# Triangular inversion in the second mixer: blocks of 16 on 128 partitions and three doublings, in place of blocks of 32 and two

## The chip, the cores and the metric

The kernel runs on one core of one Trainium2 chip, as one launch. The metric is the device time of the launch in microseconds (us): the median of the runs shown. A profile of one execution stands beside it.

## The reference

The model is two layers over 1024 tokens of width 1024; each layer is a mixer, a cross attention over a memory of 256 rows, and a squared-ReLU MLP. The second layer's mixer is a gated delta rule with 8 heads of 128 columns, worked in chunks of 64 tokens. What the change touches is the solve with a unit lower triangular matrix, one for each head and chunk:

```python
kk = jnp.einsum('nbhtd,nbhsd->nbhts', kc, kc)
lower = jnp.where(strict, bc[..., :, None] * kk * decay, 0.0)
rhs = jnp.concatenate([vc * bc[..., None], kc * (bc * jnp.exp(g))[..., None]], axis=-1)
sol = lax.linalg.triangular_solve(lower + eye, rhs, left_side=True, lower=True, unit_diagonal=True)
u_c, w_c = sol[..., :dv], sol[..., dv:]
...
v_new = u - jnp.einsum('bhtk,bhkv->bhtv', wk, S)
o = jnp.einsum('bhtk,bhkv->bhtv', qd, S) + jnp.einsum('bhts,bhsv->bhtv', att, v_new)
S = S * jnp.exp(gl)[..., None, None] + jnp.einsum('bhsk,bhsv->bhkv', kd, v_new)
```

## The kernel before

The kernel works in chunks of 128 tokens, so a head has 8 triangular matrices of 128 by 128. It forms the inverse of each, and the recurrence over the chunks then multiplies by it.

`mix_c` (L819) runs over the head pairs (0,1), (2,3), (4,5), (6,7). For a pair, `gdn_head` (L953) projects the heads' keys, queries and values on TensorE (PE; `proj`, `mm3`, L156 to L158), and `gdn_pre` (L984) convolves and scales them (VectorE, DVE, L1004 and L1008) and writes six operands of each chunk to DRAM (`Bd`), with the strictly upper triangular matrix U (the transpose of `lower`) in `Ud`. Then `gdn_inv` (L1092) inverts the pair, and for the first two pairs `gdn_rec` (L1145) runs the recurrence at once. The last two pairs run their recurrences together, as four heads, at the end; after them stand `c_gate` for the 8 heads (projections of the gate) and `mem_kv(1)` (keys and values of the memory), which need nothing of the inversion.

`gdn_inv` has two stages. In the first, the diagonal blocks of 32 by 32 of both heads are gathered from `Ud` to 64 partitions, one block on a partition (tile G, L1103). A second tile X begins as identity blocks (L1104, L1105). 31 steps of substitution follow, each of them two DVE instructions that depend on each other: a product into `pr` (L1109) and a subtraction from X (L1114). X is written to `Xd` in DRAM at the places of the diagonal blocks (L1116); the rest of `Xd` was zeroed once.

In the second stage each head is taken alone. X and U come back as 128 by 1024 tiles (L1122, L1123), the 32 by 32 blocks are transposed into Y (L1124), and two doublings follow, n = 32 and n = 64. A doubling is a chain of groups of 8 float32 matmuls with 64 moving columns, all of them through the one PSUM buffer of the tag `i`: U times X (L1129), a copy to a tile Z by ScalarE (ACT, L1132), for n = 32 alone Y times Z and a subtraction from X (L1136, L1137), then Z times Y and a subtraction from Y (L1140, L1141). So a head has five such groups. Y goes to `Bd` for the recurrence (L1088).

The order of instructions on each engine is fixed when the kernel is built: the tile framework schedules by its own timeline and mixes the inversion of one pair with the projections and convolutions of the next and with recurrences. On the chip each engine takes its instructions in that order, and one that waits holds up what is queued behind it. All DMAs here go out from the SP queue.

Of the kernel before, what the change touches and what calls it, by code (L numbers as in the profile page):

```python
# [11 lines left out]
F32 = mybir.dt.float32  # L12
# [14 lines left out]
class Model:  # L27
# [336 lines left out]
    def mix(self, l):  # L364
        if l == 0:
            with self.phase(
                dict(z=3, so=1, ml=2),
                **dict(kq=8, v=4, e=2, sp=2, sh=2, sl=1, wh=2, wl=1, A=2, ah=1, al=1, so_st=1),
            ):
                self.mix_start(l, "so", dict(M=3, W=2, V=2, N=4, C=1, st=1, gg=1, ot=1))  # L370
                self.mix_ab()
                self.out_parts(False)
                self.x_open(self.x_src)
                self.out_proj(self.a["ab_o"])
        else:
            with self.phase(
                dict(a=2, i=1, rec=2, o=1),
                **dict(X=3, Y=2, Uk=1, pr=1, B=4, y=3, S=4, on=2),
            ):
                self.first = [self.ldw(self.a["c_w"][i]) for i in (8, 0)]  # L380
                self.mix_start(l, "o", dict(raw=5, kq=2, vc=1, M=1, qe=1, ua=1, kv=2))
                self.mix_c()
                self.out_parts(True)
                self.x_open(self.x_src, (1,))
                self.out_proj(self.a["c_o"])
# [456 lines left out]
    def gdn_consts(self):  # L842
        nc, c = self.nc, self.ph

        self.cgain = c.tile([128, 1], F32, name="cgain")
        nc.sync.dma_start(out=self.cgain, in_=self.a["c_hg"])
        nc.vector.tensor_scalar_mul(self.cgain, self.cgain, 0.5)
        self.convw = c.tile([128, 96], F32, name="convw")
        nc.sync.dma_start(out=self.convw, in_=self.a["c_cw"])
        self.power = c.tile([128, 8], F32, name="power")  # L850
        nc.vector.memset(self.power[:, 0:4], 0.5)
        nc.vector.memset(self.power[:, 4:8], -0.5)

        self.zt = [c.tile([128, 1024], F32, name=f"zt{i}") for i in range(2)]
        for z in self.zt:
            nc.gpsimd.memset(z, 0.0)

        self.Ud = [self.dr.tile([8, 4 * 4128], F32, tag=f"Ud{h}", name=self.nm("Ud")) for h in range(8)]
        self.Xd = [self.dr.tile([8, 4 * 4128], F32, tag=f"Xd{h}", name=self.nm("Xd")) for h in range(4)]
        self.Bd = [self.dr.tile([8, 128, 6, 128], F32, tag=f"Bd{h}", name=self.nm("Bd")) for h in range(8)]  # L860
        for x in self.Xd:
            nc.sync.dma_start(out=self.dense(x), in_=self.zt[0].rearrange("p (c t) -> p c t", t=128))
# [2 lines left out]
        return d[:, :16384].rearrange("c (s t) -> s c t", t=128)  # L865

    def blocks(self, d):
        b = d.rearrange("c (b r) -> c b r", r=4128)[:, :, :4096]
        return b.rearrange("c b (i w) -> c b i w", w=128)[:, :, :, :32]

    def c_gate(self, h):

# [220 lines left out]
    def gdn_inv(self, heads):  # L1093

        nc = self.nc
        mm = nc.tensor.matmul
        n32 = 32 * len(heads)
        G = self.big("X")
        X = self.big("X")
        g3 = G[:n32].rearrange("p (s t) -> p s t", s=32)  # L1100
        x3 = X[:n32].rearrange("p (t c) -> p t c", t=32)
        for j, h in enumerate(heads):
            nc.sync.dma_start(out=g3[j * 32 : j * 32 + 32], in_=self.blocks(self.Ud[h]))  # L1103
        nc.gpsimd.memset(X[:n32], 0.0)  # L1104
        nc.gpsimd.memset(X[:n32, 0:1024:33], 1.0)  # L1105
        for s in range(31):
            n, w = 31 - s, s + 1
            pr = self.keep("pr", 256, F32)[:n32, : n * w].rearrange("p (t c) -> p t c", t=n)
            nc.vector.tensor_mul(  # L1109
                pr,  # L1110
                g3[:, s, s + 1 :].unsqueeze(2).broadcast_to([n32, n, w]),
                x3[:, s, :w].unsqueeze(1).broadcast_to([n32, n, w]),
            )
            nc.vector.tensor_sub(x3[:, s + 1 :, :w], x3[:, s + 1 :, :w], pr)  # L1114
        for j, h in enumerate(heads):
            nc.sync.dma_start(out=self.blocks(self.Xd[h % 4]), in_=x3[j * 32 : j * 32 + 32])  # L1116
        chunks = [slice(i * 128, i * 128 + 128) for i in range(8)]

        two = lambda t, n, i: t.rearrange("p (c b h t) -> p c b h t", c=8, b=64 // n, h=2)[:, :, :, i]
        for h in heads:  # L1120
            X, Y, U = self.big("X"), self.big("Y"), self.big("Uk")
            nc.sync.dma_start(out=X.rearrange("p (c t) -> p c t", t=128), in_=self.dense(self.Xd[h % 4]))  # L1122
            nc.sync.dma_start(out=U.rearrange("p (c t) -> p c t", t=128), in_=self.dense(self.Ud[h]))  # L1123
            nc.vector.transpose(Y, X)  # L1124
            for n, Z in zip((32, 64), self.zt):
                view = lambda t: t.rearrange("p (c b t) -> p c b t", c=8, b=64 // n)
                p = view(self.bank("i"))
                for c, s in enumerate(chunks):
                    mm(p[:, c], U[:, s], two(X, n, 0)[:, c], start=True, stop=True)  # L1129
                for b in range(64 // n):  # L1130
                    rows = slice((2 * b + 1) * n, (2 * b + 2) * n)
                    nc.scalar.copy(two(Z, n, 0)[rows, :, b], p[rows, :, b])  # L1132
                if n == 32:
                    p = view(self.bank("i"))
                    for c, s in enumerate(chunks):
                        mm(p[:, c], Y[:, s], two(Z, n, 0)[:, c], start=True, stop=True)  # L1136
                    nc.vector.tensor_sub(two(X, n, 0), two(X, n, 0), p)  # L1137
                p = view(self.bank("i"))
                for c, s in enumerate(chunks):
                    mm(p[:, c], Z[:, s], two(Y, n, 1)[:, c], start=True, stop=True)  # L1140
                nc.vector.tensor_sub(two(Y, n, 1), two(Y, n, 1), p)  # L1141
            for half in HALVES:
                self.put(h, half, 5, Y[:, half * 512 : half * 512 + 512])
# [627 lines left out]
```

## Time and profile before

| what | value |
|---|---|
| median of 3 runs | 3229.2 us (3225.93 to 3229.65) |
| the profiled execution, its own time | 3224.76 us |
| its span, first to last instruction | 3221.8 us |
| busy: PE, DVE, ACT, POOL | 95%, 66%, 41%, 29% of the span |
| mean granted TensorE clock | 0.971 |

The profile is that of one execution. The span runs from the first instruction to the last, and some 3 us of the time lie around it. Busy shares are averages over the whole kernel; the second mixer stands from about 1506 to 2300 us in the span, and the four inversions from about 1650 to 2120 us. A busy PE is not PE at its peak, and its two clock levels are 1.2 and 2.4 GHz: a granted clock of 1.00 is the upper one all the time, 0.50 the lower one.

### The profile page before, as it was taken

What the parts mean: (1) busy time and instruction counts of PE and PEld (TensorE: products, weight loads), DVE (VectorE), ACT (ScalarE), POOL (GpSimd) and SP (SyncE); (2) the same over time, 40 slices, a digit from 0 to 9 for tenths busy, and PEclk for the clock granted to TensorE, in tenths of its full rate; (3) what the DMA queues carried; (4) which work ended last, traced back from release to release, by engine and by line L of the source; (5) the groups of instructions that cost most, each with busy time, mean ns of one, the idle gap of its engine ahead of it and who ended that gap; (6) DMA issues with size and microseconds to landing.
All of it is one profiled execution on the core that took longest, in us unless ns stands there. A gap on an engine that the chain in (4) does not pass through costs nothing.

```text
span 3221.8 us, 39997 instructions
## 1 busy us (share of the span) xinstructions
PE 3045.2 (95%) x14447; PEld 2511.5 (78%) x14447; DVE 2115.9 (66%) x3342; ACT 1330.2 (41%) x2525; POOL 945.4 (29%) x725
## 2 busy tenths in 40 slices
PE   8999989999899999998988899899999899999997
PEld 6777777888678878887777788788888678878886
DVE  5567475545786667777777775654454786667777
ACT  3254464424354454433443333234333354444442
POOL 2354565313000032234343333125323100023323
PEclk9999989999899999999999899999999999999998
DMA  4333553213244464443345556665212234474432
GB/s 151 109 119 103 156 175 119 70 39 102 75 143 157 152 238 167 147 164 100 87 117 142 149 156 187 191 231 187 66 56 77 97 111 149 157 250 173 148 144 79
DMA packets 268374, 438.04 MB, mean 136 GB/s; under 512 B 38064, under 2 KB 146832, under 8 KB 261008
## 3 DMA queue, kind: packets, MB, share of 16 engines
q1 hardware_dynamic: 268176, 435.50, 41.4%
q8 instruction: 113, 1.85, 0.2%
q14 instruction: 85, 0.70, 0.1%
HBM read 300.60 MB, written 134.81 MB: 135 GB/s over the span
## 4 chain that ended last, share of the span: by engine, by line
PE 33%; DVE 9%; DMA 4%; issue 4%; POOL 1%; ACT 1%; SPq 0%; POOLq 0%; DVEq 0%; ACTq 0%
PE mm L158 3%; PE mm L157 3%; PE mm L156 3%; PE ga L1453 2%; PE ga L1454 2%; PE ga L1455 2%; PE gb L1454 1%; DVE t L1004 1%; PE gb L1455 1%; PE gb L1453 1%; PE gc L1454 1%; PE gc L1455 1%; PE gc L1453 1%; PE mm L1454 1%; PE mm L1455 1%
## 5 line engine op out<-in xcount | busy, mean ns | idle before, releaser
L156 PE MATMUL mm<-hh,wh 128*128 128x512 f32 x1248 | 503.4, 404 | 8.2 <-DVE raw L431 3.5
L157 PE MATMUL mm<-hl,wh 128*128 128x512 f32 x1248 | 504.3, 404 | 0.0
L158 PE MATMUL mm<-hh,wl 128*128 128x512 f32 x1248 | 501.9, 402 | 0.0
L150 POOL TENSOR_TENSOR wl<-wr,wh 128x1024 fp32r<-128x1024 f32 x128 | 320.6, 2506 | 448.8 <-ACT wh L149 423.4
L1445 POOL TENSOR_TENSOR r<-r,r 128x512 f32<-128x512 f32 x64 | 92.0, 1458 | 881.8 <-DVE lo L1412 881.8
L1412 DVE TENSOR_TENSOR lo<-r,hi 128x1024 fp32r<-128x1024 f32 x192 | 252.8, 1317 | 133.1 <-ACT hi L1411 132.3
L1411 ACT CAST hi<-r 128x1024 fp32r<-128x1024 f32 x192 | 201.6, 1051 | 313.7 <-PE mm L1454 126.6
L156 PEld LDWEIGHTS mm<-hh,wh 128*128 128x128 f32 x1248 | 239.4, 192 | 59.2 <-DVE raw L431 4.8
L158 PEld LDWEIGHTS mm<-hh,wl 128*128 128x128 f32 x1248 | 240.5, 193 | 48.3 <-issue 0.9
L157 PEld LDWEIGHTS mm<-hl,wh 128*128 128x128 f32 x1248 | 240.2, 192 | 48.0 <-DVE hl L474 0.4
L149 ACT CAST wh<-wr 128x1024 fp32r<-128x1024 f32 x128 | 133.8, 1046 | 213.2 <-PE mm L157 120.8
L1412 DVE TENSOR_TENSOR lo<-br,hi 128x512 fp32r<-128x512 f32 x224 | 187.0, 852 | 32.9 <-ACT hi L1411 32.8
L1453 PE MATMUL ga<-hi,hi 128*128 128x512 f32 x528 | 206.7, 392 | 1.8 <-ACT w L1550 1.0
L1455 PE MATMUL ga<-hi,lo 128*128 128x512 f32 x528 | 206.5, 391 | 0.0
L1454 PE MATMUL ga<-lo,hi 128*128 128x512 f32 x528 | 206.5, 391 | 0.0
L1411 ACT CAST hi<-br 128x512 fp32r<-128x512 f32 x224 | 133.4, 619 | 152.0 <-PE ga L1455 90.0
L1454 PE MATMUL gb<-lo,hi 128*128 128x512 f32 x432 | 169.8, 393 | 7.6 <-DVE lo L1412 7.6
L1453 PE MATMUL gb<-hi,hi 128*128 128x512 f32 x432 | 169.8, 394 | 3.6 <-ACT hi L1411 3.1
L1454 PE MATMUL gc<-lo,hi 128*128 128x512 f32 x432 | 169.1, 391 | 2.3 <-DVE lo L1412 2.3
L1455 PE MATMUL gb<-hi,lo 128*128 128x512 f32 x432 | 169.0, 392 | 0.0
L1455 PE MATMUL gc<-hi,lo 128*128 128x512 f32 x432 | 168.2, 390 | 0.0
L1453 PE MATMUL gc<-hi,hi 128*128 128x512 f32 x432 | 167.8, 390 | 0.0
(515 smaller groups left out, 7228.5 us busy)
## 6 DMA issues: line engine op xcount, KB each, us to landing
r<-in_w SPq DMA_DIRECT2D x128, 512.0 KB, 4.2
br<-hd SPq DMA_DIRECT2D x56, 1024.0 KB, 5.4
hd<-w SPq DMA_DIRECT2D x160, 256.0 KB, 3.1
B<-Bd SPq DMA_DIRECT2D x64, 384.0 KB, 4.5
hd<-t SPq DMA_DIRECT2D x64, 256.0 KB, 5.2
wr<-in_c_w SPq DMA_DIRECT2D x32, 512.0 KB, 4.3
wr<-in_ab_w SPq DMA_DIRECT2D x24, 512.0 KB, 3.6
pj<-p SPq DMA_DIRECT2D x48, 256.0 KB, 2.1
```

The lines of the kernel that those rows point to most:

```text
L149: nc.scalar.copy(hi, raw)
L150: (eng or nc.gpsimd).tensor_sub(lo, raw, hi.bitcast(F32))
L156: mm(out, w[0], x[0], start=first, stop=False)
L157: mm(out, w[0], x[1], start=False, stop=False)
L158: return mm(out, w[1], x[0], start=False, stop=last)
L1004: nc.vector.scalar_tensor_tensor(out=cv, in0=raw[:, j : j + 512], scalar=wj(j), in1=cv, op0=ALU.mult, op1=ALU.add)
L1411: nc.scalar.copy(hi, src)
L1412: (eng or nc.vector).tensor_sub(lo, src, hi.bitcast(F32))
L1445: self.nc.gpsimd.tensor_add(out[:, i : i + 512], a[:, i : i + 512], b[:, i : i + 512])
L1453: mm(ps, hi, b[k][0], start=first and k == 0, stop=False, skip_group_check=True)
L1454: mm(ps, hi, b[k][1], start=False, stop=False, skip_group_check=True)
L1455: mm(ps, lo, b[k][0], start=False, stop=last and k == 3, skip_group_check=True)
```

## The change

The diagonal blocks become 16 by 16: 8 chunks with 8 blocks, so 64 partitions for a head and 128 for a pair. The substitution has 15 steps, in tiles G and X of 256 columns that have a tag of their own (`G`, two buffers); the tag `X` goes from three buffers to two. Three doublings follow, n = 16, 32 and 64. For n = 16 the matrix U can't be used as it stands, because a product with it would bring in blocks other than those wanted, so four ACT copies place the 16 by 16 blocks in a zeroed tile `U16` (`zt[3]`), and Z is copied whole. The two first doublings have three groups of matmuls, the last one two.

```diff
-                **dict(X=3, Y=2, Uk=1, pr=1, B=4, y=3, S=4, on=2),
+                **dict(X=2, Y=2, Uk=1, G=2, pr=1, B=4, y=3, S=4, on=2),
...
-        self.zt = [c.tile([128, 1024], F32, name=f"zt{i}") for i in range(2)]
+        self.zt = [c.tile([128, 1024], F32, name=f"zt{i}") for i in range(4)]
...
-        b = d.rearrange("c (b r) -> c b r", r=4128)[:, :, :4096]
-        return b.rearrange("c b (i w) -> c b i w", w=128)[:, :, :, :32]
+        b = d.rearrange("c (b r) -> (c b) r", r=2064)[:, :2048]
+        return b.rearrange("p (i w) -> p i w", w=128)[:, :, :16]
...
-        n32 = 32 * len(heads)
-        G = self.big("X")
-        X = self.big("X")
-        g3 = G[:n32].rearrange("p (s t) -> p s t", s=32)
-        x3 = X[:n32].rearrange("p (t c) -> p t c", t=32)
+        G, X = self.keep("G", 256, F32), self.keep("G", 256, F32)
+        g3 = G.rearrange("p (s t) -> p s t", s=16)
+        x3 = X.rearrange("p (t c) -> p t c", t=16)
         for j, h in enumerate(heads):
-            nc.sync.dma_start(out=g3[j * 32 : j * 32 + 32], in_=self.blocks(self.Ud[h]))
-        nc.gpsimd.memset(X[:n32], 0.0)
-        nc.gpsimd.memset(X[:n32, 0:1024:33], 1.0)
-        for s in range(31):
-            n, w = 31 - s, s + 1
+            nc.sync.dma_start(out=g3[j * 64 : j * 64 + 64], in_=self.blocks(self.Ud[h]))
+        nc.gpsimd.memset(X, 0.0)
+        nc.gpsimd.memset(X[:, 0:256:17], 1.0)
+        for s in range(15):
+            n, w = 15 - s, s + 1
...
+            U16 = self.zt[3]
+            for b in range(4):
+                rows = slice(32 * b, 32 * b + 16)
+                nc.scalar.copy(two(U16, 16, 1)[rows, :, b], two(U, 16, 1)[rows, :, b])
             nc.vector.transpose(Y, X)
-            for n, Z in zip((32, 64), self.zt):
+            for n, Z in zip((16, 32, 64), self.zt):
...
-                    mm(p[:, c], U[:, s], two(X, n, 0)[:, c], start=True, stop=True)
-                for b in range(64 // n):
+                    mm(p[:, c], (U16 if n == 16 else U)[:, s], two(X, n, 0)[:, c], start=True, stop=True)
+                if n == 16:
+                    nc.scalar.copy(two(Z, n, 0), p)
+                for b in range(64 // n if n > 16 else 0):
...
-                if n == 32:
+                if n < 64:
```

## Rows read from the trace of the kernel before

**Rows 1.** The page, busy time by engine over the span.

```profile
PE 3045.2 (95%) x14447; PEld 2511.5 (78%) x14447; DVE 2115.9 (66%) x3342; ACT 1330.2 (41%) x2525; POOL 945.4 (29%) x725
```

**Rows 2.** Windows of 100 us: length; busy us (count) by engine; granted clock; DMA.

```profile
1640.00:1740.00 100.00, 83.94 (x367) 67.11 (x368) 83.66 (x166) 35.14 (x93) 32.20 (x27) 0.92 0.45 118
1740.00:1840.00 100.00, 87.80 (x474) 74.26 (x473) 76.54 (x160) 38.02 (x104) 33.56 (x27) 0.94 0.54 145
1840.00:1940.00 100.00, 93.43 (x550) 81.79 (x549) 74.92 (x182) 35.87 (x99) 31.22 (x27) 0.93 0.60 170
1940.00:2040.00 100.00, 94.25 (x552) 82.48 (x551) 66.27 (x144) 38.96 (x110) 30.75 (x23) 0.97 0.62 189
2040.00:2140.00 100.00, 91.20 (x512) 79.11 (x511) 46.09 (x98) 26.27 (x62) 15.98 (x9) 0.93 0.57 184
sum 500.00, PE 450.61 PEld 384.74 DVE 347.48 ACT 174.26 POOL 143.71; mean PE 90.12 PEld 76.95 DVE 69.50 ACT 34.85 POOL 28.74
```

**Rows 3.** The chain that ended last, 1640 to 2140 us, shares by line.

```profile
by line: issue 10.1%; DVE t L1004 8.0%; DMA M<-gr 7.1%; PE mm L158 5.6%; PE mm L157 5.6%; DVE pr L1109 5.5%; PE mm L156 5.4%; DVE X L1114 4.8%; PE i L1129 3.3%; DMA t<-od 2.9%; PE i L1140 2.4%; DMA X<-Xd 2.2%; DVE ua L1058 2.1%; DMA X<-Ud 2
```

**Rows 4.** Timeline of PE: start us, us, instruction, idle before and releaser.

```profile
1662.80 2.07 PE L1050 MATMUL a<-kq 128*128 128x256 f32 x4 [3.23 <-DVE s L1023]
...
1677.33 1.05 PE L1022 MATMUL a<-ones,t 128*128 128x1 f32 x8 [0.27 <-DVE kv L1073]
...
1716.22 0.47 PE L156 MATMUL mm<-hh,wh 128*128 128x512 f32 x1 [2.29 <-DVE s L1027]
...
2052.53 0.49 PE L1171 MATMUL rec<-S,B 128*128 128x128 f32 x2 [1.39 <-DVE S L1185]
```

**Rows 5.** Timeline of DVE, first pair, start of the substitution.

```profile
1658.84 0.18 DVE L1109 TENSOR_TENSOR pr<-X,X 64x31 f32<-64x31 f32 x1 [5.72 <-DMA X<-Ud]
...
1660.27 0.21 DVE L1109 TENSOR_TENSOR pr<-X,X 64x60 f32<-64x60 f32 x1
```

**Rows 6.** Waits of PE, 1640 to 2140 us: total us, times, longest.

```profile
PE i L1129 <- DMA X<-Xd: 10.2, 4, 3.2
...
PE i L1140 <- ACT zt L1132: 2.9, 1, 2.9
...
PE i L1136 <- ACT zt L1132: 0.6, 1, 0.6
...
PE i L1140 <- DVE X L1137: 0.2, 1, 0.2
```

**Rows 7.** Groups of DVE, 1640 to 2140 us: busy us, mean ns | idle before.

```profile
L1109 DVE TENSOR_TENSOR pr<-X,X 64x31 f32<-64x31 f32 (+15 forms) x124 | 55.7, 449 | 16.8 <-DMA X<-Ud 8.7 <-POOL X L1105 6.2
L1114 DVE TENSOR_TENSOR X<-X,pr 64x31 f32<-64x31 f32 (+15 forms) x124 | 48.4, 390 | 1.9
...
L1141 DVE TENSOR_TENSOR Y<-Y,i 128x512 f32<-128x512 f32 x16 | 10.9, 680 | 6.8 <-PE i L1140 6.7
```

**Rows 8.** Timeline of PE: doubling groups of 16 entries and what followed them.

```profile
1806.52 3.67 PE L1140 MATMUL i<-Y,zt 128*128 128x64 f32 x16 [2.95 <-ACT zt L1132]
1809.95 0.77 PE L156 MATMUL mm<-hh,wh 128*128 128x512 f32 x1
...
1904.49 1.89 PE L1129 MATMUL i<-X,Uk 128*128 128x64 f32 x16
1906.22 0.65 PE L1050 MATMUL a<-kq 128*128 128x256 f32 x2
```

**Rows 9.** Groups of ACT, 1640 to 2140 us, columns as in rows 7.

```profile
L1017 ACT ACTIVATE kv<-a 128x128 f32<-128x128 f32 x48 | 12.5, 274 | 3.9 <-issue 3.1 <-ACT vc L1007 0.7
```

**Rows 10.** ACT, the copy to Z: ns min/median/max, first and last start, forms.

```profile
L1132 ACT COPY zt<-i x24: 362/364/582, 1740.1 to 2108.7; 32x256 f32<-32x256 f32 x16, 64x512 f32<-64x512 f32 x8
```

**Rows 11.** POOL, the zeroing of X: ns min/median/max, first and last start.

```profile
L1104 POOL MEMSET X<- x4: 944/945/947, 1602.6 to 1959.6; 64x1024 f32 x4
```

**Rows 12.** DMA issues: count, KB each, median us to landing.

```profile
X<-Ud SPq DMA_DIRECT2D x8, 128.0 KB, 7.5
Xd<-X SPq DMA_DIRECT2D x8, 128.0 KB, 3.8
```

More of the change, by code (lines that the diff above doesn't have):

```diff
@@ L1096, in gdn_inv @@
         mm = nc.tensor.matmul
-        n32 = 32 * len(heads)
-        G = self.big("X")
-        X = self.big("X")
-        g3 = G[:n32].rearrange("p (s t) -> p s t", s=32)
-        x3 = X[:n32].rearrange("p (t c) -> p t c", t=32)
-        for j, h in enumerate(heads):
-            nc.sync.dma_start(out=g3[j * 32 : j * 32 + 32], in_=self.blocks(self.Ud[h]))
-        nc.gpsimd.memset(X[:n32], 0.0)
-        nc.gpsimd.memset(X[:n32, 0:1024:33], 1.0)
-        for s in range(31):
-            n, w = 31 - s, s + 1
-            pr = self.keep("pr", 256, F32)[:n32, : n * w].rearrange("p (t c) -> p t c", t=n)
+        G, X = self.keep("G", 256, F32), self.keep("G", 256, F32)
+        g3 = G.rearrange("p (s t) -> p s t", s=16)
+        x3 = X.rearrange("p (t c) -> p t c", t=16)
+        for j, h in enumerate(heads):
+            nc.sync.dma_start(out=g3[j * 64 : j * 64 + 64], in_=self.blocks(self.Ud[h]))
[3 more added lines that the diff above has]
+            n, w = 15 - s, s + 1
+            pr = self.keep("pr", 64, F32)[:, : n * w].rearrange("p (t c) -> p t c", t=n)
             nc.vector.tensor_mul(
                 pr,
-                g3[:, s, s + 1 :].unsqueeze(2).broadcast_to([n32, n, w]),
-                x3[:, s, :w].unsqueeze(1).broadcast_to([n32, n, w]),
+                g3[:, s, s + 1 :].unsqueeze(2).broadcast_to([128, n, w]),
+                x3[:, s, :w].unsqueeze(1).broadcast_to([128, n, w]),
             )
@@ L1115, in gdn_inv @@
         for j, h in enumerate(heads):
-            nc.sync.dma_start(out=self.blocks(self.Xd[h % 4]), in_=x3[j * 32 : j * 32 + 32])
+            nc.sync.dma_start(out=self.blocks(self.Xd[h % 4]), in_=x3[j * 64 : j * 64 + 64])
         chunks = [slice(i * 128, i * 128 + 128) for i in range(8)]
```

## The prediction

> **What bounds the kernel now.** I read the page first, then windows over the stretch that holds the four inversions, then the chain of waits, PE's own waits, and its timeline. The page says that PE is busy 95% of the span and DVE 66% [rows 1]. That is an average, so the stretch decides: from 1640 to 2140 us PE is busy 450.6 of 500 us and DVE 347.5 [rows 2]. DVE comes near to PE only in the first window (83.7 against 83.9), where the first pair's substitution runs among the convolutions of the next pair; in the last window it has 46.1 against 91.2. So the stretch is PE's, with a first fifth in which DVE is as full.
>
> How much could be won if PE never stood still? Its idle time is 500 − 450.6 = 49.4 us. The granted clock adds something: the five windows have 0.92, 0.94, 0.93, 0.97 and 0.93 [rows 2], a mean of 0.938, and with levels of 1.00 and 0.50 that is 12.4% of the time, 62 us, at the lower one. A part of the 62 us is idle itself, so at most 31 us of work is lost there. The whole slack of the stretch is at most 49 + 31 = 80 us, and whatever the change adds to PE must be found in it, or the time grows.
>
> The chain of waits looks different: the two substitution lines have 5.5% + 4.8% of it, 51.5 us of 500, and the doublings' two largest lines 3.3% + 2.4%, 28.5 us [rows 3]. A chain names one thing at a time, also where PE beside it is nearly as late; what can really be won by a faster DVE is PE's idle time that DVE ends. I went through PE's timeline in the four stretches of substitution (1658 to 1725, 1781 to 1825, 1871 to 1925, 2011 to 2053). Substitution or other work on DVE ended 13 gaps of over 0.2 us there, 0.27 to 2.29 us long, 13.5 us together; the first, the longest and the last are shown [rows 4]. The gap of 3.23 us at 1662.80 [rows 4] isn't counted, because there DVE was itself held for 5.72 us by the first product, which waited for the gather from DRAM [rows 5], and that gather stays. Other waits have nothing to do with DVE: the largest is 10.2 us in four waits for the inverse's reload [rows 6].
>
> **The change part by part.** *Substitution.* Now 248 DVE instructions of 55.7 + 48.4 = 104.1 us [rows 7]. After it 4 pairs × 15 steps × 2 = 120, of 15 to 64 elements on a partition; products of 31 and 60 elements take 0.18 and 0.21 us [rows 5], so 0.20 each, 24.0 us in all. DVE loses 80 us.
>
> *The third doubling, DVE.* Two subtractions of 128x512 for each head, like L1141 at 0.680 us [rows 7]: 16 × 0.68 = 10.9 us. DVE's net is −69 us, from 347 to about 278 us in the stretch.
>
> *The third doubling, PE.* Three more groups of 8 matmuls for each head. The group shows as 16 entries; one at full clock began at 1904.49 and the next instruction at 1906.22, so it holds PE 1.73 us [rows 8]. The number of columns (64) is the same at n = 16. That is 8 × 3 × 1.73 = 41.5 us of new PE work. If all of it were at the lower clock it would double: a group behind a gap of 2.95 us held PE from 1806.52 to 1809.95, 3.43 us [rows 8]. Groups directly behind a gap are the exception, so I take 41.5, and for the upper end five groups at the lower clock, +8.5.
>
> *ACT.* For each head four small copies of 128 columns, priced by the 128-column activations at 0.274 us [rows 9], and one whole copy of Z, by the longest copies now, 0.58 [rows 10]: 8 × (4 × 0.27 + 0.58) = 13.3 us. ACT is busy 174 of 500 us [rows 2], which hides it as work. As latency it stands in front of PE: the first group of a head waits for its four copies, 1.1 us, unless U has come earlier than X. What is queued behind that group on PE is projections and recurrence steps, and they wait with it.
>
> *POOL and DMA.* POOL clears two more tiles at the start and less of X for each pair (now 0.945 us [rows 11]); it is busy 144 of 500 us [rows 2], which covers it, and at worst it costs the 2 us of two more clears. The gather and the store of blocks keep their number of issues on SP's queue and of runs (32 × 32 of 128 bytes for a head become 64 × 16 of 64 bytes). Now they land after 7.5 and 3.8 us [rows 12]. No row has 64-byte runs; the bounds are the same time or half of it, and I take the same, because the count of runs is unchanged. Two buffers of X in place of three cost nothing: G no longer uses them, two heads need two, and the four-head recurrence, which takes both X and both Y, has had only two Y all along.
>
> *The sum.* New PE work, +41.5. Relief where DVE held PE: of the 13.5 us of gaps, and of 1.7 us of slow clock behind the longest (a group behind a gap lost 3.43 − 1.73), 15.2 us at most and 0 at least; with DVE at 56% in place of 69% I take 13. New work that falls into a gap that stays: PE is idle a tenth of the stretch, so a tenth of 41.5, −4 (bounds 0 and 25, the latter some two thirds of the idle time that is left). New waits: the hand-offs of the two doublings cost PE 2.9 + 0.6 + 0.2 us in all [rows 6], for three of them in each head, 0.15 each; three more in each head make 24 × 0.15 = 3.7, of which I take 3 (bounds 0 and 28, see the last rival). Together 41.5 − 13 − 4 + 3 = +27.5 us. The profiled execution took 3224.8 us, so 3252.3, rounded to 3252. That execution lies 4.4 us under the median of the runs shown and 1.2 us under the fastest of them; against the median my forecast is +0.7%.
>
> **Rivals.** *Faster: DVE's chain is the bound.* If the chain of waits is taken at its word, the substitution falls from 51.5 to 51.5 × 24.0/104.1 = 11.9 us, a saving of 39.6. The doublings' shown lines are 32 groups, 55.4 us, of which 28.5 are on the chain, 51%; 24 new groups at that share cost 21.4, and the new subtractions at the substitution's share (51.5/104.1) 5.4. The net is −12.8 us: 3212. For it speaks the first window, in which DVE is as full as PE; against it the three last windows, where PE has 91% and more. It decides if PE's idle time and slow clock fall by more than the 41.5 us that PE gains in work, half of all the slack there is. Chance 0.20.
>
> *No change that can be measured: the new groups fill gaps.* If 25 us of them fall where PE stood idle, the sum is 41.5 − 13 − 25 + 0 = +3.5: 3228. Gaps filled also keep the clock up: the group behind a gap ran at half speed, the other one at full [rows 8]. The Trainium skill (TensorE: Matmul & The Clock Gate, Part 1: The HAM clock gate) says the same as a rule: the slow clock is the state TensorE falls into, and activity releases it, so that each gap closed would also give back the slow work behind it. The trace agrees with 3.43 against 1.73 us. Against the rival: the gaps that are left are mostly waits for DMAs and recurrence steps, in front of which the order on PE is fixed. Chance 0.16.
>
> *Slower still: the longer chain holds PE.* A head's chain grows by 1.1 + 3 × 1.73 + 0.58 + 2 × 0.68 = 8.2 us through one PSUM buffer. If a quarter of the 24 new hand-offs held PE as long as the longest now (2.9 us [rows 6]) and left it at the lower clock for one group (1.7 more), that is 6 × 4.6 = 28 us: 41.5 − 13 − 4 + 28 gives 3277. For it speaks that in the last pair nothing but gate projections is left to mix in; against it that such a hold happened once among 24. Chance 0.14.
>
> **How the numbers follow.** The forecast has 0.50. A measurement of this kernel can tell about 0.2%, 6.5 us, from no change: that puts the first rival (0.20) under faster, the second (0.16) under same, and the forecast and the third rival under slower, 0.64. The forecast's own range is 3237 (all relief, more of the work in gaps) to 3268 (no relief). The whole range goes down to 3212, which leaves out the lower half of the first rival, and up to 3275, which leaves out half of the last one: less than 2 in 10.
>
> **What would show it.** In the profile after: 120 substitution instructions on 128 partitions with a mean near 0.20 us (more would be VectorE held by something else); 64 groups of L1129's kind of lines at 1.73 us where there were 40; from 1640 us to the end of the last inversion PE's busy time up by about 40 us, DVE's down by about 70, PE's waits for DVE in the substitutions nearly gone, and those for the reload of X as before or about 1 us longer. The prediction is wrong if PE's idle time in the stretch falls under 15 us, or if new groups stand where PE idled before.

## The result and the profile after

The changed kernel takes 3253.4 us (median of 4 runs, 3248.18 to 3260.46) against 3229.4 for the kernel before: a ratio of 1.0075, interval 1.0057 to 1.0093. The forecast was 3252. That it was met to 2 us says less than it seems to. The runs below show that the new PE work was sized right, that the relief set against it did not come as forecast, and that the order of instructions alone moves either kernel by up to 14 us.

The profiled execution took 3260.5 us, 7 over its median, with a span of 3258.5; that of the kernel before was 4.7 under its median. So the two spans differ by 36.7 us where the medians differ by 24.0. First the page's row of busy times, the answer to [rows 1]:

```profile
PE 3089.5 (95%) x14831; PEld 2558.9 (79%) x14831; DVE 2066.5 (63%) x3230; ACT 1343.5 (41%) x2565; POOL 934.6 (29%) x727
```

PE has 44.3 us more busy time and DVE 49.4 less. PE's idle time, span less busy, went from 176.6 to 169.0. So the lost time is busy time of PE; no large wait has appeared (the longest in the stretch of the inversions is 4.7 us, below). The windows over the stretch of the inversions, as in [rows 2]:

```profile
1640.00:1740.00 100.00, 86.42 (x437) 72.44 (x435) 67.60 (x132) 38.64 (x107) 31.56 (x30) 0.93 0.43 114
1740.00:1840.00 100.00, 93.00 (x513) 79.93 (x512) 63.63 (x133) 39.53 (x100) 30.18 (x29) 0.92 0.53 149
1840.00:1940.00 100.00, 95.86 (x603) 84.90 (x603) 61.90 (x141) 40.94 (x123) 25.11 (x23) 0.97 0.55 145
1940.00:2040.00 100.00, 96.18 (x624) 86.02 (x623) 61.75 (x152) 39.42 (x118) 28.28 (x25) 0.98 0.64 190
2040.00:2140.00 100.00, 94.95 (x526) 82.26 (x525) 38.92 (x54) 22.22 (x45) 16.27 (x8) 0.95 0.46 140
sum 500.00, PE 466.42 PEld 405.55 DVE 293.81 ACT 180.76 POOL 131.40; mean PE 93.28 PEld 81.11 DVE 58.76 ACT 36.15 POOL 26.28
```

PE is denser in each window (466.4 us of 500 against 450.6), but the same 500 us hold less of the mixer's work: the last doubling group ends at 2169 us in place of 2115. From 1640 us to that end PE is busy 490.4 us in place of 428.4 and idle 38.1 in place of 46.9. The forecast expected some 40 us more busy time there; the 62 include other work, because the stretch is 53 us longer. PE's groups of the doublings, 1640 to 2170 us, after the change (matmuls as entries, two for each; busy us, mean ns | idle before):

```profile
L1144 PE MATMUL i<-Y,zt 128*128 128x64 f32 x384 | 49.9, 279 | 1.4 <-DVE X L1141 1.4
L1131 PE MATMUL i<-X,Uk 128*128 128x64 f32 x256 | 33.7, 283 | 4.3 <-DVE Y L1145 4.3
L1140 PE MATMUL i<-zt,Y 128*128 128x64 f32 x256 | 31.6, 271 | 1.0 <-ACT zt L1136 1.0
L1131 PE MATMUL i<-X,zt 128*128 128x64 f32 x128 | 18.0, 296 | 5.8 <-DMA X<-Xd 3.9 <-ACT wh L149 1.9
```

That is 1024 entries, 64 groups of 16, as forecast. Their busy time is 133.2 us, 2.08 for each. The same groups in the kernel before, 1640 to 2140 us:

```profile
L1129 PE MATMUL i<-X,Uk 128*128 128x64 f32 x256 | 33.9, 284 | 12.7 <-DMA X<-Xd 10.2 <-DMA Uk<-Ud 2.5
L1140 PE MATMUL i<-Y,zt 128*128 128x64 f32 x256 | 33.4, 280 | 3.2 <-ACT zt L1132 2.9 <-DVE X L1137 0.2
L1136 PE MATMUL i<-zt,Y 128*128 128x64 f32 x128 | 15.8, 270 | 0.6 <-ACT zt L1132 0.6
```

These are 40 groups of 83.1 us, again 2.08 each. The 24 new groups thus hold 50.1 us of busy time, where the forecast took 24 × 1.73 = 41.5, the price of a group that ran at the upper clock [rows 8]. Such a group's own record is 1.89 us (its end overlaps the next instruction), so the lower clock and split groups add 0.19 to each on average. Of the 8.6 us over the forecast, 3.8 are this overlap of the records and 4.6 the lower clock and the splits.

DVE's groups, 1640 to 2180 us, and the gather and store of the blocks:

```profile
L1107 DVE TENSOR_TENSOR pr<-G,G 128x15 f32<-128x15 f32 (+7 forms) x60 | 21.4, 356 | 14.9 <-DMA G<-Ud 13.9
L1145 DVE TENSOR_TENSOR Y<-Y,i 128x512 f32<-128x512 f32 x24 | 16.4, 682 | 6.8 <-PE i L1144 6.7
L1112 DVE TENSOR_TENSOR G<-G,pr 128x15 f32<-128x15 f32 (+7 forms) x60 | 15.0, 250 | 1.2
L1141 DVE TENSOR_TENSOR X<-X,i 128x512 f32<-128x512 f32 x16 | 10.9, 683 | 6.6 <-PE i L1140 6.4
```

```profile
Xd<-G SPq DMA_DIRECT2D x8, 64.0 KB, 2.7
G<-Ud SPq DMA_DIRECT2D x7, 64.0 KB, 6.3
```

The substitution has 120 instructions, as said, but 36.4 us in place of 24.0. Both transfers land about 1 us sooner than in [rows 12], within the bounds. Last, PE's waits, 1640 to 2140 us:

```profile
PE a L1050 <- DVE s L1023: 4.7, 1, 4.7
PE i L1131 <- DMA X<-Xd: 3.9, 1, 3.9
...
PE i L1131 <- DVE Y L1145: 1.7, 1, 1.7
...
PE i L1140 <- ACT zt L1136: 0.7, 1, 0.7
...
PE i L1144 <- DVE X L1141: 0.6, 1, 0.6
```

In the four stretches of substitution, one gap over 0.2 us ended by DVE is left (1.01 us) where the forecast counted 13; a second one (0.63 us) is a hand-off of a doubling, a kind that its count left out. As before, one more stands directly behind DVE's own wait for the gather and isn't counted (4.7 us, first row). The stretches are also shorter, 66 us together in place of 207. Over 1560 to 2340 us, PE's gaps of over 0.2 us ended by DVE fell from 31.4 to 22.9 us.

The hand-offs of all doublings cost 1.7 + 0.7 + 0.6 = 3.0 us in this view, but it ends before the last inversion does. Up to 2170 us they are 4.3 + 1.0 + 1.4 = 6.7 us (the rows of groups above) against 3.7 before [rows 6], 3 us more. The longest, in the last head, and the window behind it:

```profile
2155.90 3.67 PE L1131 MATMUL i<-X,Uk 128*128 128x64 f32 x16 [2.61 <-DVE Y L1145]
```

```profile
2153.00:2170.00 17.00, 13.81 (x64) 13.44 (x64) 8.44 (x19) 4.57 (x10) 0.69 (x1) 0.50 0.32 109
```

### The profile page after: what moved, and what is told of

The parts are those of the page before. It is cut to its first block, busy times and chain, and to the rows that moved or that the text cites. A ratio compares the mean times of both kernels' runs of the same rounds, so it can differ in the third digit from the quotient of the medians.

```text
span 3258.5 us, 40678 instructions
## 1 busy us (share of the span) xinstructions
PE 3089.5 (95%) x14831; PEld 2558.9 (79%) x14831; DVE 2066.5 (63%) x3230; ACT 1343.5 (41%) x2565; POOL 934.6 (29%) x727
## 5 line engine op out<-in xcount | busy, mean ns | idle before, releaser
L1458 PE MATMUL mm<-lo,hi 128*128 128x512 f32 x400 | 159.5, 399 | 9.5 <-DVE lo L1416 9.5
```

The source lines that it names most:

```text
L1458: mm(ps, hi, b[k][1], start=False, stop=False, skip_group_check=True)
```

## The experiments

The forecast's theory: new PE work costs its duration, less what falls into gaps, and relief of DVE is worth the gaps that DVE ended. The rivals of the first four runs make DVE's chain, or the chain of hand-offs, the bound. A third one came up after those runs: that work at these places costs more than its duration, because of PE's clock or of what is queued behind. What the twelve runs showed is in the tables at the end of this section.

**The two halves taken apart.** First the new substitution with two doublings only:

```diff
-            for n, Z in zip((16, 32, 64), self.zt):
+            for n, Z in zip((32, 64), self.zt):
```

> The changed kernel without its doubling n = 16: the four copies to U16, the three groups of matmuls, the copy to Z and the two subtractions of each head are left out, so the inverse lacks the off-diagonal halves of the 32 by 32 blocks and the output is not the reference's. VectorE has about 80 us less to do than in the kernel before and TensorE the same. Theory (TensorE is the bound, and what a faster VectorE can give back are the gaps that VectorE ended, 13.5 us, with the slow clock behind them): 13 us less than before, about 3216 us, and not below 3212. Rival (VectorE's chain is the bound, with the substitution's 51.5 us of the chain): 40 us less, about 3190 us.

Measured: 3202.0 us, ratio 0.9918 (0.9902 to 0.9933), 27.7 below the kernel before (3229.75 in the runs beside it). That is twice the relief of the forecast, and between the theory (3216) and the rival (3190); neither was met. The page and the window of 1640 to 2140 us say where it came from:

```profile
PE 3025.4 (95%) x14447; PEld 2499.5 (78%) x14447; DVE 2062.5 (64%) x3214; ACT 1329.0 (42%) x2525; POOL 936.9 (29%) x727
```

```profile
1640.00:2140.00 500.00, 456.89 (x2602) 395.10 (x2603) 310.42 (x665) 187.01 (x511) 141.56 (x120) 0.96 0.58 171
```

PE has as many instructions as before (14447), and its busy time fell by 19.8 us, while its idle time stayed (174.5 against 176.6). The granted clock of the stretch is 0.96, where the mean of [rows 2] was 0.938. In this trace PE was busy at the lower clock for 117.3 us, in that of the kernel before for 150.9; half of the difference, 16.8 us, is what the same work saved. The mean granted clock of the six runs is 0.976, of the 45 runs of the kernel before 0.972. So the relief came mostly as work at the upper clock, and the forecast counted 1.7 us of that. It isn't all owed to DVE: from 1560 to 2340 us the lower clock held 72 us before and 44 here, and put down to the longest wait of PE beside each slow stretch, those at waits for DMA and ACT went from 44 to 21 us, those at waits for DVE from 27 to 24.

Then the other half, the old substitution with a third doubling whose U16 is all zeros:

```diff
+                nc.scalar.mul(two(U16, 16, 1)[rows, :, b], two(U, 16, 1)[rows, :, b], 0.0)
...
-            for n, Z in zip((32, 64), self.zt):
+            for n, Z in zip((16, 32, 64), self.zt):
```

> The kernel before, with its blocks of 32 and 31 steps, and a third doubling in front of the two, fed with zeros (U16 is U times 0.0), so that it changes nothing in the result. It adds what the change adds (24 groups of matmuls, 32 small and 8 whole copies, 16 subtractions) and takes nothing away. Theory: 24 groups of 1.73 us are 41.5 us, a tenth of them in gaps, 3 us of new waits: 40 us more than before, about 3270 us (3262 to 3278). Rival (the groups cost TensorE only what the doublings have of the chain, 51%, and the subtractions 5.4): 27 us more, about 3256 us. If the two terms simply add up, this run and the one without the third doubling give the change's 24 us together.

Measured: 3294.7 us, ratio 1.0200 (1.0177 to 1.0222): +65, above both theories. With the −27.7 of the other half that makes +37, so the two halves don't simply add up to the +24 of the change. One place of it, PE's doubling groups by time, and two windows there:

```profile
2089.13 2.56 PE L1146 MATMUL i<-Y,zt 128*128 128x64 f32 x16 [2.27 <-DVE X L1143]
...
2092.86 3.51 PE L1133 MATMUL i<-X,Uk 128*128 128x64 f32 x16
...
2097.04 3.68 PE L1146 MATMUL i<-Y,zt 128*128 128x64 f32 x16
2101.59 3.68 PE L1133 MATMUL i<-X,zt 128*128 128x64 f32 x16
...
2106.01 3.60 PE L1142 MATMUL i<-zt,Y 128*128 128x64 f32 x16
...
2115.67 3.51 PE L1133 MATMUL i<-X,Uk 128*128 128x64 f32 x16
...
2125.07 1.89 PE L1142 MATMUL i<-zt,Y 128*128 128x64 f32 x16
```

```profile
2100.00:2120.00 20.00, 19.74 (x91) 19.04 (x91) 5.76 (x11) 5.90 (x19) 2.05 (x2) 0.50 0.43 138
2120.00:2140.00 20.00, 20.00 (x113) 17.45 (x112) 9.74 (x16) 3.83 (x6) 2.39 (x1) 0.97 0.33 111
```

After a gap of 2.27 us at a hand-off of the n = 32 doubling, the groups from 2092.86 on take 3.5 to 3.7 us each up to 2119, and 1.89 again at 2125. The new n = 16 groups of the next head, from 2101.59 on, fall into this slow time. In the window of 2100 to 2120 PE is busy 19.74 us of 20 at a granted clock of 0.50: half of what PE could have done in that window is lost with no wait to be seen.

**What PE work costs.** In the changed kernel, the n = 16 groups issued twice; and, for comparison, as much PE time in dense matmuls in front of the same groups:

```diff
+                for c, s in enumerate(chunks * (2 if n == 16 else 1)):
+                    c %= 8
```

> The changed kernel with each matmul of the doubling n = 16 issued twice, the second pass over the same PSUM columns, so that the result stays and no hand-off to another engine is added. Theory (TensorE's time is what counts): another 24 x 1.73 = 41.5 us, less a tenth that falls in gaps: 37 us more than the changed kernel, about 3290 us. Rival (what costs is the chain of hand-offs, TensorE's own time by half): 21 us more, about 3275 us; if the matmuls were hidden in gaps altogether, about 3253 us.

```diff
+            for _ in range(k):
+                mm(bank, self.h[0][0][0][:, :128], self.h[0][0][0], start=True, stop=True)
```

> The changed kernel with 23 matmuls of 128x512 per head put in front of the three n = 16 groups (8, 8 and 7), 184 in all, of the kind of the projections (0.2275 us each where they run back to back in the trace of before), results overwritten: 41.9 us of PE work, as much as the 41.5 us of the run that issued the n = 16 groups twice (+56). Theory A (short float32 groups cost more than their 1.73 us, because of what they do to the clock; dense work costs its own time, less what falls into gaps): +37 to +42 us over the changed kernel, 3291 to 3295. Theory B (any PE work at these places costs a third more than its duration, because of what is queued behind it): +56, 3309.

Measured: 3309.3 us (+56 over the changed kernel) and 3308.6 (+55). The dense work was to cost 37 to 42 us if the short float32 groups were dear by their kind; it costs the same, so the excess isn't theirs. (Eight of the 184 dense matmuls ran early, at 1514.6 us; the others stand in front of their groups.) The number is theory B's, but its claim, a third on top of any work at these places, isn't shown by it: both runs also have an order of their own, and the tables at the end of this section put the excess in different places. The two pages, first the doubled groups, then the dense work:

```profile
PE 3129.5 (95%) x15215; PEld 2603.6 (79%) x15215; DVE 2072.8 (63%) x3230; ACT 1345.3 (41%) x2565; POOL 933.0 (28%) x727
```

```profile
PE 3119.1 (94%) x15015; PEld 2585.4 (78%) x15015; DVE 2061.9 (62%) x3230; ACT 1344.2 (41%) x2565; POOL 933.9 (28%) x727
```

Neither has less idle time than the changed kernel (176.6 and 185.1 us against 169.0 as planned and 176.7 on average over three orders of it). The added work did not fill gaps.

**One group in three, and ACT's copies.** The X group of n = 16 replaced by a DVE transpose of Y, and, apart from it, the changed kernel without U16:

```diff
-                if n < 64:
+                if n == 32:
...
+                if n == 16:
+                    nc.vector.transpose(X, Y)
```

> The changed kernel with one group of matmuls less: in the doubling n = 16 only Y is brought up to date by matmuls, and X is then made from Y by VectorE's transpose of 32 by 32 blocks (1.245 us), in place of a group (1.73 us) and a subtraction (0.68 us). Theory: TensorE has 8 x 1.73 = 13.8 us less, a tenth of it was in gaps: 12 us less than the changed kernel, about 3241 us, still slower than before. Rival (VectorE's chain): VectorE has 8 x 0.56 = 4.5 us more and TensorE's 13.8 count by half: 4 us less at most, about 3249 to 3254 us.

```diff
-                    mm(p[:, c], (U16 if n == 16 else U)[:, s], two(X, n, 0)[:, c], start=True, stop=True)
+                    mm(p[:, c], U[:, s], two(X, n, 0)[:, c], start=True, stop=True)
```

> The changed kernel without U16 and its four ScalarE copies per head: the n = 16 groups take U itself, so the inverse is not the reference's. PE's and VectorE's work is the same. Theory A (the copies' 9.4 us lie beside other work): within 4 us of the changed kernel, 3250 to 3254. Theory B (each head's first group waits for the copies and PE is held, falling to the lower clock): 8 heads by 1.1 us and one group at the lower clock, 1.7 us, some 20 us less, 3233.

Measured: 3240.8 us, ratio 1.0036 (1.0022 to 1.0050), which is 12.7 below the changed kernel and still above the kernel before; and 3252.3, 1.1 below the changed kernel. Both are the numbers of the first theory: a group left out saves about its duration, and the 20 us that the copies were to cost by theory B aren't there. A few us for the copies can't be excluded, since a new order alone moves the time by that much (below).

**Relief without new PE work.** The old blocks of 32, with four heads substituted together on 128 partitions; first for the heads 0 to 3, then for all:

```diff
-            self.gdn_inv(pair)
-            if pair[1] < 4:
-                self.gdn_rec(pair, oq)
+            if pair[1] == 3:
+                self.gdn_inv((0, 1, 2, 3))
+                self.gdn_rec((0, 1), oq)
+                self.gdn_rec((2, 3), oq)
+            elif pair[1] > 3:
+                self.gdn_inv(pair)
```

> The kernel before, with the heads 0 to 3 substituted together on 128 partitions: one chain of 62 VectorE instructions in place of two, at the same duration each. PE's work is the same; VectorE loses 62 instructions of the 248, a quarter of 104.1 us, 26 us. Theory A (taking substitution off VectorE pays at the rate of the run without the third doubling, 27.7 us for 67.7 us of VectorE): -10.6 us, 3219. Theory B (only the counted gaps of PE pay, 13 us for 80): -4 us, 3226. Against both: the first pair's doublings and recurrence now wait for the heads 2 and 3; if PE runs out of other work in that time, 3235 and more.

> As the last, and the heads 4 to 7 substituted together too: VectorE loses half of the 104.1 us, 52 us. Theory A: -21 us, 3208. Theory B: -8 us, 3221. Against both: the doublings of four heads, 20 groups of 1.73 us, then stand behind the last substitution with only recurrences and gate projections to mix with; if each of the 10 groups that lose their cover holds PE for 2.9 us more, +29, 3240 and more.

Measured: 3259.8 us (+31) and 3246.2 (+18). Both miss theories A and B, though DVE has 62 and 124 instructions fewer, and lie where the remarks against both put them (3235 and 3240 or more). PE's largest wait, 1600 to 2300 us, of the first, the same wait in the kernel before, and the window of 1640 to 2140 us of the first:

```profile
PE a L1053 <- DVE s L1026: 19.0, 6, 5.6
```

```profile
PE a L1050 <- DVE s L1023: 4.1, 3, 3.2
```

```profile
1640.00:2140.00 500.00, 442.90 (x2355) 379.12 (x2354) 316.84 (x675) 170.36 (x466) 134.00 (x112) 0.91 0.54 153
```

These waits of a head's key products for DVE's copy of its sums of squares (L1053 and L1026 here, L1050 and L1023 before) grew by 15 us, and the granted clock of the stretch fell from 0.94 to 0.91. In the second run they are 15.6 us. The remark against both had named PE running out of other work; the largest wait is one for a result of DVE. The grouping cost more than the shorter substitution gave; why the copies came later wasn't tried. A change of grouping is a change of order, and this raised a question about all the runs: how much is any new order worth?

**The order by itself.** Two edits that change no engine's work: the two stores of an inverse issued in the other order, and the second head of a pair doubled ahead of the first. The framework then plans anew; between 1,400 and 2,400 of PE's some 12,900 rows stand elsewhere.

```diff
-            for half in HALVES:
+            for half in HALVES[::-1]:
                 self.put(h, half, 5, Y[:, half * 512 : half * 512 + 512])
```

> The kernel before with the two stores of each inverse to DRAM (the halves, L1088) issued in the other order. Every engine does the same instructions as before; but the tile framework plans anew, and some 1,420 of PE's 12,882 rows stand elsewhere in its order. Theory A (the order that the plan happens to give is worth tens of us, which would also account for the +31 and +18 of the runs with four heads substituted together): the time differs from 3229 by 10 us or more, either way. Theory B (the times follow from the work, and a shuffled order of it is worth little): 3229, within 6 us.

> The same swap of the two stores in the changed kernel; some 2,380 of PE's rows stand elsewhere, no work is added. Theory A: differs from 3253 by 10 us or more, either way. Theory B: 3253, within 6 us.

```diff
-        for h in heads:
+        for h in heads[::-1]:
             X, Y, U = self.big("X"), self.big("Y"), self.big("Uk")
```

> The kernel before with the second head of each pair taken through the doublings ahead of the first. Same work; some 1,820 of PE's rows stand elsewhere. Theory A: differs from 3229 by 10 us or more, either way, and not by as much as the last kernels in the same direction. Theory B: 3229, within 6 us.

> The same swap of the heads in the changed kernel; some 2,420 of PE's rows stand elsewhere. Theory A: differs from 3253 by 10 us or more, either way; if A holds, the changed kernel and the kernel before overlap over their orders. Theory B: 3253, within 6 us, and the change costs 24 us in every order.

| order | kernel before, us | changed kernel, us |
|---|---|---|
| as planned | 3229.4 | 3253.4 |
| stores swapped | 3215.4 (ratio 0.9964, 0.9950 to 0.9978) | 3264.9 (1.0116, 1.0101 to 1.0131) |
| heads swapped | 3233.6 (1.0017, 1.0005 to 1.0028) | 3257.9 (1.0100, 1.0084 to 1.0115) |
| mean | 3226.1 | 3258.7 |

Ratios are to the kernel before as planned. The same work in another order moves by up to 14 us, and the same swap helps one kernel and harms the other; so theory A holds for the stores, and theory B for the heads (4 us each). The +31 of the run with the heads 0 to 3 together lies outside that. Yet no order of the changed kernel is as fast as the slowest of the kernel before. Over the orders the change costs 3258.7 − 3226.1 = 32.6 us; with a scatter of 9.6 and 5.8 us over three orders each, that is uncertain by some 6 us. Row by row it is 24.0, 49.6 and 24.2. Of the kernels that leave nothing out, the kernel before with its stores swapped is the fastest.

The tables for the profiled executions: idle is span less PE's busy time, from the pages; slow is PE's busy time while the granted clock stood at 0.50, from the trace's record of the clock; work is busy less half of slow, an estimate of what the same instructions hold PE at the upper clock. So a span is work, plus half of slow, plus idle.

| run | median, us | span | PE busy | of it slow | PE work | PE idle | DVE busy | clock |
|---|---|---|---|---|---|---|---|---|
| before | 3229.4 | 3221.8 | 3045.2 | 150.9 | 2969.7 | 176.6 | 2115.9 | 0.971 |
| before, stores swapped | 3215.4 | 3217.8 | 3042.8 | 148.3 | 2968.7 | 175.0 | 2112.7 | 0.971 |
| before, heads swapped | 3233.6 | 3220.7 | 3034.5 | 126.7 | 2971.1 | 186.2 | 2114.4 | 0.975 |
| changed | 3253.4 | 3258.5 | 3089.5 | 165.3 | 3006.9 | 169.0 | 2066.5 | 0.968 |
| changed, stores swapped | 3264.9 | 3262.7 | 3079.8 | 143.0 | 3008.3 | 182.9 | 2078.2 | 0.972 |
| changed, heads swapped | 3257.9 | 3252.5 | 3074.2 | 132.7 | 3007.8 | 178.3 | 2074.1 | 0.973 |

| run | median, us | span | PE busy | of it slow | PE work | PE idle | DVE busy | clock |
|---|---|---|---|---|---|---|---|---|
| two doublings only | 3202.0 | 3199.9 | 3025.4 | 117.3 | 2966.7 | 174.5 | 2062.5 | 0.977 |
| third doubling only | 3294.7 | 3291.8 | 3103.9 | 185.5 | 3011.2 | 187.9 | 2126.6 | 0.965 |
| n = 16 groups twice | 3309.3 | 3306.1 | 3129.5 | 161.7 | 3048.7 | 176.6 | 2072.8 | 0.969 |
| dense work added | 3308.6 | 3304.2 | 3119.1 | 136.8 | 3050.7 | 185.1 | 2061.9 | 0.971 |
| transpose for a group | 3240.8 | 3243.7 | 3069.9 | 151.6 | 2994.1 | 173.8 | 2086.0 | 0.971 |
| no copies | 3252.3 | 3250.3 | 3083.7 | 150.1 | 3008.6 | 166.6 | 2067.3 | 0.971 |
| four heads, 0 to 3 | 3259.8 | 3264.1 | 3063.4 | 178.2 | 2974.3 | 200.7 | 2096.8 | 0.965 |
| four heads, all | 3246.2 | 3243.0 | 3057.5 | 164.7 | 2975.2 | 185.5 | 2072.2 | 0.969 |

The column of work is steady: over its three orders the kernel before has 2968.7 to 2971.1 us, the changed kernel 3006.9 to 3008.3, while their busy times differ by 11 and 15 us. What differs between the orders is the loss to the lower clock and the idle time. The kernel before loses 63 to 75 us to the lower clock (half of slow) and idles for 175 to 186.

## Why the prediction was right, and where its steps were not

*What bounds the kernel: right.* The stretch was PE's, and the time followed PE's work. The first rival, that DVE's chain is the bound, is refuted by the changed kernel's time in all three orders; its own condition, that idle and slow time fall by more than 41.5 us, wasn't near.

*The new PE work: right in size.* The forecast has 24 × 1.73 = 41.5 us. In the tables, PE's work rises by 37.8 us with the change (averages over the orders), by 41.4 with the third doubling alone, and over the changed kernel by 41.0 with the groups doubled and 43.0 with the dense work; with one group in three left out it falls by 13.6, where 13.8 were forecast.

*What falls into gaps: wrong, though small.* The forecast took 4 us off. The two runs with work added to the changed kernel have 0 and 8 us more idle time than its average, not less. The change itself took 2.5 us of idle time away on average over the orders, or 6.5 if only the part with the mixer is taken (from 1500 us to 880 us before the end), and DVE's shorter waits are in that. So the second rival, which needs 25, fails on its own condition.

*The excess of the added work.* The two runs with +56 and +55 are 51 and 50 us over the average of the changed kernel's orders. In the spans it is 48.2 and 46.3: for the doubled groups 41.0 us of work, 7.3 of lower clock and no idle time, for the dense work 43.0 of work, 5.1 less lost to the lower clock and 8.3 of idle time. Each of these differences is no larger than what separates two orders of one kernel, so a price above the duration isn't shown, nor is a few us of it excluded. The stretch's mean rate, PE busy for 450.6/500 = 0.90 of it at a granted clock of 0.938 [rows 2], would make 41.5/(0.90 × 0.938) = 49 us. That comes near to the sum, but not to its parts, since neither run shows both kinds of loss.

*The relief: the step that did not hold.* The forecast took 13 us from gaps that DVE ended. Those waits shrank by 8 us (from 31.4 to 22.9 as planned, and by as much on average over the orders), and PE's idle time as a whole by the 2.5 us above, 6.5 in the part with the mixer, where the forecast's terms make −13 − 4 + 3 = −14. The run with two doublings lies 24 below the mean of the kernel before over its orders, yet only 5 of the 20 us in its span are idle time. 12 are less loss to the lower clock, for which the sum had 1.7, behind the longest gap alone, and 3 less work. And in the changed kernel the gain at the clock is gone: its orders lose 73.5 us to the lower clock on average, those of the kernel before 71.0. The relief that was measured without the third doubling thus doesn't carry over to the kernel with it; why the lower clock comes back there isn't settled.

*New waits: 3 us, as forecast,* though its working has a slip: the five groups of a head have four hand-offs among them, not three, which makes 24 × 3.7/32 = 2.8 in place of 3.7.

*The sum.* The averages of the traces over the orders are +37.8 of work, +2.5 lost to the lower clock and −2.5 of idle time, +37.8 in all; the medians make that +32.6. The forecast of +27.5 lies under both, because it counted on 14 us less idle time, of which 2.5 came, 6.5 in the mixer. That the order as planned measured +24.0, and the forecast of 3252 was met to 2 us, is luck on top of a right mechanism: with the stores swapped in both kernels the same change costs 49.6. The forecast also started from an execution 4.7 us under the median.

*Substitution on DVE: count right, duration wrong.* 36.4 us in place of 24.0, and DVE's busy time fell by 49.4 us, not 69. Of the 120 instructions, 110 take 0.2 us; the other ten, of 0.53 to 2.36 us, hold 11.9 of the 12.4 us too many (last section). What they cost in time wasn't tried; DVE isn't the bound.

*ACT: right.* Hidden as work, and as latency nothing that stands out of the scatter of the orders (3252.3 without the copies).

*The reload of X: wrong.* It was to be as before or 1 us longer; it fell from 10.2 us in four waits to 3.9 in one. One reason that the traces offer is that a shorter substitution and store (2.7 us in place of 3.8) bring X sooner while PE has more to do; this wasn't tried.

*The third rival, longer holds,* supposed six holds of 2.9 us with slow work behind. In the changed kernel as planned one occurred, in the last head: 2.61 us, with the lower clock from 2153 to 2170 us. In the run with the third doubling alone, where DVE was still loaded, a gap of 2.27 us had 30 us of slow clock behind it. There the third doubling cost 65 us; between the two runs with the new substitution (3202.0 and 3253.4) it cost 51. So the rival's mechanism exists, and its size was too large for this kernel.

## What to carry to other kernels

Where an engine is busy for nine tenths of a stretch and other work is queued behind in a fixed order, price new work of that engine at its full duration, and don't expect gaps to take it in: here 41 and 43 us of added work left the idle time where it was, or 8 us higher. What relief of another engine gives in idle time is bounded by the gaps that it ended (8 us here, of 13 counted on), and doesn't tell what the clock will do. Split a measured difference into work at the upper clock, loss to the lower clock and idle time before it is given a cause. And where a planner sets the order anew, run an edit that changes the order alone, before a difference of some 10 us is explained.

## What the runs showed of the hardware

*A small VectorE operation can last as long as a GpSimd operation beside it.* VectorE and GpSimd in the changed kernel by time, in the first pair's and second pair's substitutions (start us, us):

```profile
1675.20 0.69 DVE L431 SCALAR_TENSOR_TENSOR raw<-mm,yy 128x512 f32<-128x512 f32 x1
1675.81 1.83 DVE L1107 TENSOR_TENSOR pr<-G,G 128x28 f32<-128x28 f32 x1
...
1768.78 0.22 DVE L1112 TENSOR_TENSOR G<-G,pr 128x64 f32<-128x64 f32 x1
1769.04 2.36 DVE L1107 TENSOR_TENSOR pr<-G,G 128x63 f32<-128x63 f32 x1
```

```profile
1675.19 2.40 POOL L150 TENSOR_TENSOR wl<-wr,wh 128x1024 fp32r<-128x1024 f32 x1 [6.21 <-ACT wh L149]
...
1768.94 2.38 POOL L150 TENSOR_TENSOR wl<-wr,wh 128x1024 fp32r<-128x1024 f32 x1 [5.67 <-ACT wh L149]
```

A product of 28 elements takes 1.83 us and ends at 1677.64, POOL's subtraction at 1677.59; one of 63 elements takes 2.36 and ends at 1771.40, POOL's at 1771.32. All ten long ones of the substitution end within 0.1 us of a POOL instruction with two tensor inputs. The first row, one of whose inputs comes from PSUM, isn't held. The Trainium skill (GPSIMD Engine Reference, 1. Specifications) says that GpSimd shares its SBUF interfaces with VectorE, and that VectorE instructions with two SBUF inputs contend for them; the trace agrees, and here the small one lasted to the end of the large one. Not every GpSimd instruction does this: nine of the small products and subtractions ran wholly within a `pow` of GpSimd on 128x4 or 128x8 (1.0 and 1.6 us, also with two tensor inputs) and took 0.18 to 0.23 us.

*The lower clock can last while PE is busy.* In the run with the third doubling alone PE stood at 0.50 with 19.74 us of 20 busy, among 64-column and 128-column float32 groups. The Trainium skill (TensorE: Matmul & The Clock Gate, Part 1: The HAM clock gate) has activity release the slow clock; in that window activity was there and the clock did not rise until 2121 us. PE's work changed just before: at 2120.23 us the projections of 512 columns began again. Whether that ended it was not tried.
